# A gain vector brought to 128 partitions by two TensorE products instead of by a broadcasting load

## The chip, the cores and the metric

The kernel runs on one core of a Trainium2 chip. The metric is the device time of one execution in microseconds. The kernel before took 854.26 us, the median of three runs (853.2 to 855.99). One execution was also recorded by the hardware profiler; it took 853.36 us.

## The reference

One layer of an encoder trunk over 1536 tokens of 1024 features, in three groups of 512 tokens (a prompt of 1024 and a sample of 512):

```
h = rmsnorm(x, norm_g)            # x * rsqrt(mean(x*x) + 1e-6) * norm_g, per token over 1024 features
p = h @ w_in                      # 1024 x 4096, its columns split among three mixers
y = concat(conv branch, gated spatial branch, two-way recurrence)   # 256 + 256 + 512 wide
x = x + y @ w_out
out = rmsnorm(x, final_norm_g)
```

The change concerns norm_g alone, a vector of 1024 numbers that multiplies every token's features. Tokens lie on the 128 partitions while it is applied, so each partition needs the whole vector.

## The kernel before, in words

All products are made in float32 precision: a factor is split into a rounded part (hi, wh, hh) and a remainder (lo, wl, hl), and three products of such parts are summed (lines 204 to 206). ACT makes the rounded part, POOL or DVE the remainder.

At the start, `local_main` has SP issue the loads in this order: the first two chunks of 128 tokens (x00, x01), gb, two tiles of weights (wr), chunks 2 and 3, another weight tile, then the second group of tokens and the small parameter rows. The tile gb, 128 x 1024, is filled by one load that reads norm_g once for each partition, 512 KB (line 421).

The routine `prep` then turns token chunks into columns for the projection. For each chunk, ACT squares the tokens and sums them (`squares`, line 288), POOL makes the reciprocal root (lines 117 and 118), DVE multiplies the chunk by it and by gb (line 302), TensorE transposes it in eight blocks through two banks (tx, line 312), ACT evicts each bank rounded (hh, line 315) and DVE makes the remainder (hl, line 316). In between, `w_split` rounds the weights on ACT (wh, line 122) and makes their remainder on POOL (wl, line 123).

`prep` begins with `warm(18)`: 18 products of the identity with itself into a bank that nobody reads (line 216). Two more stand between the first two chunks. The first projection (pglu, lines 204 to 206) works on half a group, 256 tokens, at a time, so that it can start after two chunks; the transposes of chunks 2 and 3 stand in the middle of its products.

On ACT, DVE and POOL the instructions around the change run in the order in which the code is written. TensorE's stream is arranged by the framework's scheduler from the code and from what each instruction depends on. Each engine works through its own stream strictly in order and waits for the others by semaphores.

Of the kernel before, what the change touches and what calls it, by code (L numbers as in the profile page):

```python
# [11 lines left out]
F32 = mybir.dt.float32  # L12
# [3 lines left out]
AF = mybir.ActivationFunctionType  # L16
# [4 lines left out]
P = 128  # L21
DM = 1024
KT = DM // P
GRP = 512
# [9 lines left out]
WARM = (18, 2, 0)  # L34
# [21 lines left out]
def trunk_kernel(ctx, tc, x_prompt, x_sample, norm_g, w_in, conv_w, conv_b, conv_ln_g, conv_ln_b,  # L56
                 conv_pw, sgu_ln_g, sgu_ln_b, sgu_w, sgu_b, lb_fwd, lb_bwd, hgrn_norm_g, w_out,
                 final_norm_g, masks, y_prompt, y_sample):
    nc = tc.nc
    act = nc.scalar.activation  # L60
    dve = nc.vector
# [17 lines left out]
    def pj_t(name):  # L79
        return ps_pj.tile([P, GRP], F32, tag="pj", name=name)  # L80

    def tp_t(name):
        return ps_tp.tile([P, GRP], F32, tag="tp", name=name)

    def sc_t(name):
        return ps_sc.tile([P, NCH, P], F32, tag="sc", name=name)
# [4 lines left out]
    def uo_t(name):  # L91
        return ps_uo.tile([P, NCH, P], F32, tag="uo", name=name)
# [19 lines left out]
    def rstd(out, in_, n, mul=None):  # L112

        if mul is None:
            pool_e.tensor_scalar(out=out, in0=in_, scalar1=EPS, scalar2=None, op0=ALU.add)
        else:
            pool_e.tensor_scalar(out=out, in0=in_, scalar1=mul, scalar2=EPS, op0=ALU.mult, op1=ALU.add)
        pool_e.tensor_tensor(out=out, in0=out, in1=mexp[:, :n], op=ALU.pow)
# [93 lines left out]
    def warm(n):  # L212

        t = uo_t("warm").rearrange("p c n -> p (c n)")
        for _ in range(n):
            nc.tensor.matmul(t[:, :P], ident, ident, start=True, stop=True)
# [60 lines left out]
    def load_x(g, c, alloc):  # L277
        xt = alloc([P, DM], f"x{g}{c}")
        nc.sync.dma_start(xt, xsrc[g][c * P:(c + 1) * P, :])
        return xt  # L280

    def prep(xs, junk_t, gb):

        sts = {}

        def squares(g, c):
            st = sts[g, c] = const.tile([P, 1], F32, tag="st_x", name=f"st{g}{c}", bufs=4)
            act(junk_t(f"jx{g}{c}"), xs[g][c], AF.Square, accum_out=st)

        def by_pool(g, c):  # L290
            return g and c % 2 == 1

        def gained(g, c):
            pool_e.tensor_tensor(out=xs[g][c], in0=xs[g][c], in1=gb, op=ALU.mult)

        def scaled(g, c):
            xt, st = xs[g][c], sts[g, c]
            rstd(st, st, 1, 1.0 / DM)
            if by_pool(g, c):
                dve.tensor_scalar(out=xt, in0=xt, scalar1=st, scalar2=None, op0=ALU.mult)  # L300
            else:
                dve.scalar_tensor_tensor(out=xt, in0=xt, scalar=st, in1=gb, op0=ALU.mult, op1=ALU.mult)

        def turned(g, c):
            if c == 0:
                hts[g] = [[big.tile([P, 4, GRP], F32R, tag="H", name=f"h{e}{g}{a}") for a in range(2)] for e in "hl"]
            his, los = hts[g]
            xt = xs[g][c]
            for a in range(2):
                tp = tp_t(f"tx{g}{c}{a}") if a == 0 else sc_t(f"tx{g}{c}{a}").rearrange("p c n -> p (c n)")  # L310
                for k in range(4):
                    nc.tensor.transpose(tp[:, k * P:(k + 1) * P], xt[:, (4 * a + k) * P:(4 * a + k + 1) * P], ident)
                tp3 = tp.rearrange("p (k t) -> p k t", k=4)
                hi, lo = his[a][:, :, c * P:(c + 1) * P], los[a][:, :, c * P:(c + 1) * P]
                act(hi, tp3, AF.Copy)
                dve.tensor_tensor(out=lo, in0=tp3, in1=hi.bitcast(F32), op=ALU.subtract)
            ready[g] = c + 1

        warm(WARM[0])
        squares(0, 0)  # L320
        scaled(0, 0)
        squares(0, 1)
        scaled(0, 1)
        w_split()
        turned(0, 0)
        warm(WARM[1])
        turned(0, 1)
        warm(WARM[2])
        squares(0, 2)
        scaled(0, 2)  # L330
        squares(0, 3)
        scaled(0, 3)
        w_split()
        yield 4
        turned(0, 2)
        yield 2
        turned(0, 3)
        yield 1
        rest = [(g, c) for g in range(1, NG) for c in range(NCH)]
        for i in range(len(rest) + 2):  # L340
            if i < len(rest):
                squares(*rest[i])
            if 1 <= i <= len(rest):
                scaled(*rest[i - 1])
            if i < len(rest) and by_pool(*rest[i]):
                gained(*rest[i])
            if i >= 2:
                turned(*rest[i - 2])
            yield PACE
# [32 lines left out]
    def local_main(l1, accs):  # L382

        glus = [[l1.tile([P, len(gs) * GRP + 2 * PAD], F32, tag=f"glu{si}", name=f"glu{si}{i}", bufs=2)
                 for si, gs in enumerate(seqs)] for i in range(2)]
        gb = l1.tile([P, DM], F32, tag="gb", name="gb")

        def sg_t(name):
            return l1.tile([P, GRP], F32, tag="sg", name=name, bufs=3)

        def where(g):
            return (0, g) if g < 2 else (1, 0)

        def glu_pair(i, g, parts=(slice(0, GRP),)):
            sg = sg_t(f"sglu{i}{g}")

            def val_done(pj):
                si, j = where(g)
                dve.tensor_tensor(out=glus[i][si][:, PAD + j * GRP:PAD + (j + 1) * GRP], in0=pj, in1=sg, op=ALU.mult)

            pg, pv = pj_t(f"pglu{i}{g}"), pj_t(f"pval{i}{g}")
            for part in parts:
                last = g == NG - 1 and part.stop == GRP
                project(A_GLU + i, g, "", lambda pj: act(sg, pj, AF.Sigmoid), pg, part)
                if last:
                    w_split()
                project(A_VAL + i, g, "", val_done, pv, part)
                if last:
                    w_split()

        with tc.tile_pool(name="xp", bufs=1) as xp:
            def x_t(shape, name):
                return xp.tile(shape, F32, tag="x", name=name, bufs=9)

            def junk_t(name):
                return xp.tile([P, DM], BF16, tag="junk", name=name, bufs=2)

            xs = [[] for _ in range(NG)]
            xs[0].append(load_x(0, 0, x_t))
            xs[0].append(load_x(0, 1, x_t))  # L420
            nc.sync.dma_start(gb, norm_g.broadcast_to((P, DM)))
            w_load()
            w_load()
            for c in range(2, NCH):
                xs[0].append(load_x(0, c, x_t))
            w_load(x_t([P, KT, P], "wr2"))
            xs[1] = [load_x(1, c, x_t) for c in range(NCH)]
            rows = xp.tile([N_ROWS, P], F32, tag="rows", name="rows")
            for r0, src in ((R_NG, norm_g[0]), (R_CB, conv_b[0]), (R_CLG, conv_ln_g[0]), (R_CLB, conv_ln_b[0]),
                            (R_SLG, sgu_ln_g[0]), (R_LBF, lb_fwd[0]), (R_LBB, lb_bwd[0]), (R_HNG, hgrn_norm_g[0]),  # L430
                            (R_CW, conv_w[0].rearrange("a b -> (a b)"))):
                n = src.shape[0] // P
                nc.sync.dma_start(rows[r0:r0 + n, :], src.rearrange("(r j) -> r j", j=P))

            for i in range(2):
                for si, gs in enumerate(seqs):
                    pool_e.memset(glus[i][si][:, :PAD], 0.0)
                    pool_e.memset(glus[i][si][:, PAD + len(gs) * GRP:], 0.0)
            with tc.manual_schedule(engines={mybir.EngineType.Activation, mybir.EngineType.DVE,
                                             mybir.EngineType.Pool}):  # L440
                task = prep(xs, junk_t, gb)
                next(task)
                xs[2] = [load_x(2, c, x_t) for c in range(NCH)]
                spawn(task)
                for g in range(NG):
                    glu_pair(0, g, (slice(0, GRP // 2), slice(GRP // 2, GRP)))
            pp = tp_t("pp")
            nc.tensor.transpose(pp[:, :N_ROWS], rows, ident[:N_ROWS, :N_ROWS])
            dve.tensor_copy(par, pp[:, :N_ROWS])
        with tc.tile_pool(name="l2", bufs=1, reuse_waits="tile") as l2:  # L450
            with tc.manual_schedule(engines={mybir.EngineType.Activation, mybir.EngineType.DVE,
                                             mybir.EngineType.Pool}):
                local_rest(l2, accs, glus, glu_pair, where)
# [721 lines left out]
```

## Time and profile before

| | |
|---|---|
| time, median of three runs | 854.26 us (853.2 to 855.99) |
| the profiled execution | 853.36 us |
| its span, first to last instruction | 851.5 us |
| PE (TensorE products) busy | 824.1 us, 97% |
| DVE, ACT, POOL busy | 503.2, 348.6, 279.1 us (59%, 41%, 33%) |
| moved by DMA | 55.57 MB, mean 65 GB/s |
| mean granted TensorE clock | 0.993 |

A product of two float32 tiles shows as two records on PE, a transpose or a product of rounded parts as one. Records overlap, since products are pipelined; the spacing of their starts tells how fast they go, not the length of one. The time of a load is from its issue on SP's queue (SPq) to the moment at which a waiting engine goes on.

### The profile page before, as it was taken

The page shows a single profiled execution, that of the slowest core. Times are in us where ns is not written, and L with a number is a line of the kernel's source. Part 1 is how long each engine was busy: PE and PEld are TensorE (multiplying, and loading weights), DVE is VectorE, ACT ScalarE, POOL GpSimd, SP SyncE. Part 2 cuts the span into 40 slices and gives each one's busy share as a digit, 9 for nine tenths or more (in the row PEclk, how much of TensorE's full clock was granted, in tenths as well). Part 3 has the DMA queues.
Part 4 walks back from the last instruction along what each step waited for, and adds up shares of the span by engine and source line. Part 5 has one row for each costly group of instructions (what it writes and reads, how often), then busy time and mean ns, then how long its engine had stood idle before and what let it go on. Part 6 is the DMA issues. An engine that isn't in the chain of part 4 may idle for free.

```text
span 851.5 us, 17505 instructions
## 1 busy us (share of the span) xinstructions
PE 824.1 (97%) x7249; PEld 705.2 (83%) x7249; DVE 503.2 (59%) x1024; ACT 348.6 (41%) x707; POOL 279.1 (33%) x288
## 2 busy tenths in 40 slices
PE   7999999999999999999999999999999779999996
PEld 6998998787888889988878888998887667888886
DVE  4737789756323588631498748873227998443332
ACT  5724546541344354422345434442224555222221
POOL 5826766986142321220222032103113540101111
PEclk9999999999999999999999999999999899999999
DMA  7301201121020200101101011002212261334421
GB/s 273 138 16 42 75 2 49 50 64 62 25 62 13 75 27 3 49 28 38 50 27 39 2 38 48 19 2 63 75 36 87 79 210 51 126 130 144 146 99 50
DMA packets 56929, 55.57 MB, mean 65 GB/s; under 512 B 2875, under 2 KB 46226, under 8 KB 56850
## 3 DMA queue, kind: packets, MB, share of 16 engines
q1 hardware_dynamic: 56850, 54.45, 19.7%
q8 instruction: 57, 0.93, 0.5%
q14 instruction: 22, 0.18, 0.1%
HBM read 41.86 MB, written 12.58 MB: 64 GB/s over the span
## 4 chain that ended last, share of the span: by engine, by line
PE 83%; DVE 10%; ACT 2%; DMA 1%; POOL 1%; issue 1%; SPq 0%; POOLq 0%; ACTq 0%; DVEq 0%
PE pf L204 5%; PE po L1060 5%; PE po L1058 5%; PE pf L206 5%; PE pf L205 5%; PE po L1059 5%; DVE Q L765 4%; PE o L957 3%; PE pq L204 2%; DVE K L765 2%; PE sc L790 2%; PE pq L205 2%; PE pq L206 2%; PE U L890 2%; PE pg L204 2%; PE pg L205 2%
## 5 line engine op out<-in xcount | busy, mean ns | idle before, releaser
L123 POOL TENSOR_TENSOR wl<-wr,wh 128x512 fp32r<-128x512 f32 x64 | 85.5, 1349 | 162.4 <-ACT wh L122 162.4
L475 DVE SCALAR_TENSOR_TENSOR ca<-glu,par,ca 128x512 f32<-128x512 f32 x120 | 80.6, 748 | 0.0
L1058 PE MATMUL po<-woh,yh 128*128 128x512 f32 (+1 forms) x200 | 77.6, 388 | 0.8 <-ACT yh L1038 0.8
L1060 PE MATMUL po<-woh,yl 128*128 128x512 f32 (+1 forms) x200 | 76.5, 383 | 1.5 <-DVE yl L1039 1.5
L204 PE MATMUL pf<-hh,wh 128*128 128x512 f32 x192 | 76.8, 400 | 0.0
L1059 PE MATMUL po<-wol,yh 128*128 128x512 f32 (+1 forms) x200 | 76.2, 381 | 0.0
L206 PE MATMUL pf<-hh,wl 128*128 128x512 f32 x192 | 75.0, 391 | 0.0
L205 PE MATMUL pf<-hl,wh 128*128 128x512 f32 x192 | 74.8, 390 | 0.0
L771 ACT ACTIVATE kc<-K 128x512 f32<-128x512 f32 x84 | 56.4, 674 | 43.1 <-DVE K L765 40.4
L500 POOL TENSOR_TENSOR part<-part,pr 128x512 f32<-128x512 f32 x54 | 68.7, 1301 | 13.0 <-ACT pr L499 13.0
L765 DVE TENSOR_TENSOR Q<-Q,T 128x256 f32<-128x256 f32 x144 | 69.7, 525 | 2.0 <-ACT q L801 0.8
L765 DVE TENSOR_TENSOR K<-K,T 128x256 f32<-128x256 f32 x144 | 61.1, 465 | 5.8
L122 ACT ACTIVATE wh<-wr 128x512 fp32r<-128x512 f32 x64 | 39.0, 627 | 54.7 <-PE pf L205 20.6
L709 DVE TENSOR_SCALAR Q<-Q,oml,lbt 128x512 f32<-128x512 f32 x24 | 17.8, 742 | 64.8 <-ACT Q L706 64.8
L1064 DVE TENSOR_TENSOR yx<-po,yx 128x512 f32<-128x512 f32 (+1 forms) x25 | 16.7, 670 | 58.7 <-PE po L1060 58.7
L1060 PEld LDWEIGHTS po<-woh,yl 128*128 128x128 f32 x200 | 37.6, 188 | 9.2 <-DVE yl L1039 2.0
L1058 PEld LDWEIGHTS po<-woh,yh 128*128 128x128 f32 x200 | 37.6, 188 | 7.8 <-ACT yh L1038 0.9
L1059 PEld LDWEIGHTS po<-wol,yh 128*128 128x128 f32 x200 | 37.7, 188 | 6.8
L206 PEld LDWEIGHTS pf<-hh,wl 128*128 128x128 f32 x192 | 36.0, 188 | 7.8
L1076 POOL TENSOR_TENSOR stf<-stf 128x1 f32<-128x1 f32 x12 | 3.1, 261 | 119.0 <-ACT yx L1065 119.0
L204 PEld LDWEIGHTS pf<-hh,wh 128*128 128x128 f32 x192 | 36.1, 188 | 7.1
L205 PEld LDWEIGHTS pf<-hl,wh 128*128 128x128 f32 x192 | 36.1, 188 | 6.9
(366 smaller groups left out, 2265.1 us busy)
## 6 DMA issues: line engine op xcount, KB each, us to landing
wr<-in_w_in_dram SPq DMA_DIRECT2D x62, 256.0 KB
out_dram<-yx SPq DMA_DIRECT2D x24, 256.0 KB
yx<-yd SPq DMA_DIRECT2D x12, 448.0 KB
x<-in_x_prompt_dram SPq DMA_DIRECT2D x8, 512.0 KB
wor<-in_w_out_dram SPq DMA_DIRECT2D x8, 512.0 KB
yx<-in_x_prompt_dram SPq DMA_DIRECT2D x8, 512.0 KB
yd<-yc SPq DMA_DIRECT2D x12, 256.0 KB
x<-in_x_sample_dram SPq DMA_DIRECT2D x4, 512.0 KB
```

Of the source, the lines that this page charges most:

```text
L122: act(hi, src, AF.Copy)
L123: pool_e.tensor_tensor(out=lo, in0=src, in1=hi.bitcast(F32), op=ALU.subtract)
L204: nc.tensor.matmul(pj[:, part], hi[:, k, :], hh, start=k == 0, stop=False)
L205: nc.tensor.matmul(pj[:, part], hi[:, k, :], hl, start=False, stop=False)
L206: nc.tensor.matmul(pj[:, part], lo[:, k, :], hh, start=False, stop=k == KT - 1)
L475: dve.scalar_tensor_tensor(out=acc, in0=src, scalar=col(R_CW + 2 * t + i), in1=acc, op0=ALU.mult, op1=ALU.add)
L500: pool_e.tensor_tensor(out=parts[g], in0=parts[g], in1=pr, op=ALU.add)
L765: dve.tensor_tensor(out=x, in0=x, in1=y, op=ALU.mult)
L771: act(view(kc, 0, [[2 * m, n2], [m, 2], [1, m]]), view(K, 0, [[2 * m, n2], [GRP + m, 2], [1, m]]), AF.Copy)
L1058: nc.tensor.matmul(po, yh[:, k, :], hi[:, ns], start=k == 0, stop=False)
L1059: nc.tensor.matmul(po, yh[:, k, :], lo[:, ns], start=False, stop=False)
L1060: nc.tensor.matmul(po, yl[:, k, :], hi[:, ns], start=False, stop=k == KT - 1)
```

## The change

A row tile, grow, of one partition with 1024 numbers is loaded with norm_g (4 KB), as the second load instead of the third, between x00 and x01. A row of 128 ones is set by DVE. Two products of the ones, as the stationary factor, with a half of grow each, put 512 features of the vector on all 128 partitions of a bank (gp); they have one row of contraction each. ACT copies each bank into a half of gb. The 18 warm-up products are written as nine before and nine behind these products.

```diff
-    def prep(xs, junk_t, gb):
+    def prep(xs, junk_t, gb, ones, grow):
...
-        warm(WARM[0])
+        warm(WARM[0] // 2)
+
+        for a in range(2):
+            gp = tp_t(f"gp{a}")
+            nc.tensor.matmul(gp, ones, grow[:, a * GRP:(a + 1) * GRP], start=True, stop=True)
+            act(gb[:, a * GRP:(a + 1) * GRP], gp, AF.Copy)
+        warm(WARM[0] // 2)
         squares(0, 0)
         scaled(0, 0)
...
             xs[0].append(load_x(0, 0, x_t))
+            grow = xp.tile([1, DM], F32, tag="grow", name="grow")
+            nc.sync.dma_start(grow, norm_g[0:1, :])
             xs[0].append(load_x(0, 1, x_t))
-            nc.sync.dma_start(gb, norm_g.broadcast_to((P, DM)))
+            ones = xp.tile([1, P], F32, tag="ones", name="ones")
+            dve.memset(ones, 1.0)
             w_load()
             w_load()
```

The streams as the engines get them differ from the text of the code on TensorE. Its stream at the start of the program, before (warm is the warm-up product, tx a transpose, pglu the first projection):

```order
L1171 UNCONDITIONAL_BRANCH
L216 MATMUL warm<-ident 128x128 x18
L312 MATMUL tx_197<-ident,x_109 128x128 x4
L312 MATMUL tx_204<-ident,x_109 128x128 x4
L216 MATMUL warm<-ident 128x128 x2
L312 MATMUL tx_214<-ident,x_111 128x128 x4
L312 MATMUL tx_221<-ident,x_111 128x128 x4
L204 MATMUL pglu_260<-hh_193,wh_183 128x256
```

and now, where gp is a product of the ones with half the vector:

```order
L1180 UNCONDITIONAL_BRANCH
L323 MATMUL gp_165<-grow,ones 128x512
L323 MATMUL gp_168<-grow,ones 128x512
L216 MATMUL warm<-ident 128x128 x18
L312 MATMUL tx_207<-ident,x_109 128x128 x4
L312 MATMUL tx_214<-ident,x_109 128x128 x4
L216 MATMUL warm<-ident 128x128 x2
L312 MATMUL tx_224<-ident,x_113 128x128 x4
L312 MATMUL tx_231<-ident,x_113 128x128 x4
L204 MATMUL pglu_270<-hh_203,wh_193 128x256
```

Both gp products stand ahead of all 18 warm-up products, not between two halves of them; what follows is in the order of before.

ACT's stream at the start of the program, before:

```order
L288 ACT_TABLE_LOAD
L288 ACTIVATE jx_172,st_171<-x_109 128x1024
L288 ACTIVATE jx_178,st_177<-x_111 128x1024
L122 ACTIVATE wh_183<-wr_114 128x512
L122 ACTIVATE wh_183<-wr_116 128x512
L315 ACTIVATE hh_193<-tx_197 128x4x128
```

and now:

```order
L324 ACT_TABLE_LOAD
L324 ACTIVATE gb<-gp_165 128x512
L324 ACTIVATE gb<-gp_168 128x512
L288 ACTIVATE jx_182,st_181<-x_109 128x1024
L288 ACTIVATE jx_188,st_187<-x_113 128x1024
L122 ACTIVATE wh_193<-wr_117 128x512
L122 ACTIVATE wh_193<-wr_119 128x512
L315 ACTIVATE hh_203<-tx_207 128x4x128
```

The two copies of gp stand ahead of the squares of the first chunk.

## Rows read from the trace of the kernel before

**Rows 1.** The page: busy engines, and the chain that ended last by engine

```profile
PE 824.1 (97%) x7249; PEld 705.2 (83%) x7249; DVE 503.2 (59%) x1024; ACT 348.6 (41%) x707; POOL 279.1 (33%) x288
...
PE 83%; DVE 10%; ACT 2%; DMA 1%; POOL 1%; issue 1%; SPq 0%; POOLq 0%; ACTq 0%; DVEq 0%
```

**Rows 2.** The chain in order of time, 8 to 22 us: start, us, what

```profile
2.57 7.92 DMA wr<-in_w_in_dram
...
10.52 0.63 ACT wh L122
...
13.91 1.27 ACT jx L288 x3
...
17.08 2.30 DVE x L302
...
19.52 1.07 PE tx L312 x8
```

**Rows 3.** Timeline of ACT, first 30 us: start, us, instruction, [idle before, releaser]

```profile
4.45 1.06 ACT L288 ACTIVATE jx<-x 128x1024 bf16<-128x1024 f32 x1 [2.44 <-DMA x<-in_x_prompt_dram]
...
5.73 1.06 ACT L288 ACTIVATE jx<-x 128x1024 bf16<-128x1024 f32 x1
...
9.46 0.63 ACT L122 ACTIVATE wh<-wr 128x512 fp32r<-128x512 f32 x1 [2.58 <-DMA wr<-in_w_in_dram]
10.52 0.63 ACT L122 ACTIVATE wh<-wr 128x512 fp32r<-128x512 f32 x1 [0.43 <-DMA wr<-in_w_in_dram]
11.06 2.04 ACT L315 ACTIVATE hh<-tx 128x512 fp32r<-128x512 f32 x4
12.96 1.08 ACT L288 ACTIVATE jx<-x 128x1024 bf16<-128x1024 f32 x1
```

**Rows 4.** Timeline of POOL, first 30 us

```profile
5.68 0.19 POOL L117 TENSOR_SCALAR st<-st 128x1 f32<-128x1 f32 x1 [4.10 <-ACT jx L288]
5.95 0.56 POOL L118 TENSOR_TENSOR st<-st,mexp 128x1 f32<-128x1 f32 x1
```

**Rows 5.** Timeline of DVE, first 30 us

```profile
8.30 2.48 DVE L302 SCALAR_TENSOR_TENSOR x<-x,st,gb 128x1024 f32<-128x1024 f32 x2 [7.45 <-DMA gb<-in_norm_g_dram]
```

**Rows 6.** Timeline of PE, first 14 us

```profile
1.64 6.81 PE L216 MATMUL warm<-ident 128*128 128x128 f32 x36 [1.64 <-POOL ident masks.py:199]
9.64 1.09 PE L312 MATMUL tx<-ident,x 128*128 128x128 f32 x8 [1.19 <-DVE x L302]
10.57 0.61 PE L216 MATMUL warm<-ident 128*128 128x128 f32 x4
11.02 1.04 PE L312 MATMUL tx<-ident,x 128*128 128x128 f32 x8
```

**Rows 7.** Windows over the warm-up: stretch, length, PE busy (records), PEclk, DMA, GB/s

```profile
1.63:7.00 5.37, 5.37 (x25) 1.00 0.90 294
7.00:8.50 1.50, 1.45 (x13) 1.00 0.96 265
```

**Rows 8.** Timeline of SP's queue: issues of the first loads

```profile
0.72 0.86 SPq L279 DMA_DIRECT2D x<-in_x_prompt_dram  x2
1.63 0.42 SPq L421 DMA_DIRECT2D gb<-in_norm_g_dram  x1
2.10 1.08 SPq L178 DMA_DIRECT2D wr<-in_w_in_dram  x2
```

**Rows 9.** Windows of one us, columns as in rows 7

```profile
1.00:2.00 1.00, 0.36 (x1) 1.00 0.22 33
2.00:3.00 1.00, 1.00 (x6) 1.00 0.74 238
3.00:4.00 1.00, 1.00 (x7) 1.00 1.02 401
...
6.00:7.00 1.00, 1.00 (x7) 1.00 0.83 195
```

**Rows 10.** Waits over the whole span: us in total, times, longest

```profile
DVE ga L626 <- ACT ga L625: 9.1, 4, 4.3
```

More of the change, by code (lines that the diff above doesn't have):

```diff
@@ L440, in local_main @@
                                              mybir.EngineType.Pool}):
-                task = prep(xs, junk_t, gb)
+                task = prep(xs, junk_t, gb, ones, grow)
                 next(task)
```

## The prediction

> **What bounds the kernel now.** The page first: PE is busy for 97% of the span and the chain that ended last is 83% PE and 1% DMA [rows 1]. Then the chain in order of time over the first 22 us [rows 2], because the change sits there: it starts with the loads of the first projection weights, a wait of 7.92 us on wr until 10.52, and goes on over ACT's rounding of them (wh), ACT's evictions of the transposes (hh), the squares of the third token chunk (jx), and POOL and DVE's scaling, to the transposes at 19.52; from there PE works nearly without a gap. 7.92 of 851.5 us is 0.9%, so this one wait is nearly all the DMA in the whole chain. Behind it everything is written in program order on engines that wait for one another, and nothing waits for a clock on the wall. A shift of the opening therefore goes to the end one for one, in both directions.
>
> The opening itself is read engine by engine. ACT: x00 has landed at 4.45, squares of chunks 0 and 1 at 4.45 and 5.73, then idle until the weights land (9.46, 10.52), then four evictions and at 12.96 the squares of chunk 2 [rows 3]. POOL makes the first rstd by 6.51 [rows 4]. DVE could scale x00 then, but waits for the broadcast vector gb until 8.30 [rows 5]. PE runs 18 warm-up products (36 records) from 1.64 to 8.45 and the first transposes at 9.64 [rows 6]. The 12.96 is my mark: the third chunk's squares head the chain from there [rows 2], so its shift is the shift of the end.
>
> **What the change takes away.** The 512 KB of gb were third on SP's queue, ahead of both weight tiles [rows 8]. At 195 to 401 GB/s, the ends of the slices where it could run [rows 9], they are 1.3 to 2.7 us, by which the weights land sooner, and DVE loses its wait from 6.51 to 8.30. Alone that would be a gain of at most about 2 us. It counts only if what replaces gb is there in time.
>
> **What it puts in.** One 4 KB load, DVE's memset of 128 ones, four PE records and two ACT copies. The order of instructions decides: on PE both products stand ahead of all 18 warm-up products, and on ACT both copies stand ahead of the first squares. So PE no longer starts at 1.64 but when grow lands, and the 36 warm records, until now finished in an idle stretch, are queued behind the products and in front of the first transposes.
>
> Landing of grow: second on the queue, issued about 1.16, behind x00. Of x00's 524 KB, 33 + 238 KB had moved by 3.0 us and at 401 GB/s the rest by 3.63 [rows 9]; ACT saw it at 4.45 [rows 3], 0.8 us later. In line behind it I take 4.7. From the other side: x00's first bytes move about 1 us after its issue at 0.72 (33 GB/s in the second microsecond) [rows 8, 9]; a load that waited for nobody would be seen at 1.16 + 1.0 + 0.8 = 3.0. Later than 5.7 it can't be, since a 512 KB load in that place was seen by then [rows 3]. [...]
>
> Products: of the warm records 25 lie in 1.63 to 7.00, 215 ns each, and 13 in 7.00 to 8.50, 112 ns each [rows 7]. PEclk reads 1.00 in both, so the level has to be read from the spacing: it is half speed (1.2 GHz) first, then 2.4 GHz, and the engine had streamed without a gap since 1.64 when it rose. A product of 512 columns is also two records, of four times the columns: 0.86 us each at the lower level, 0.45 at the upper. PE now begins cold at 4.7: four records are 3.44 us, to 8.14. The first product is ready at 6.42 and the second at 8.14, each plus an estimated 0.2 to drain. The copies go by ACT's evictions of the same 128x512, four in 2.04 us, so 0.5 to 0.6 each [rows 3]: 6.6 to 7.2 and 8.35 to 8.95.
>
> ACT and DVE behind that: squares at 8.95 and 10.23 (pitch 1.28), the two wh from 11.5 to 12.75 (the weights have long landed). rstd of chunk 0: POOL begins 1.23 after the squares do and takes 0.83 [rows 4], 11.0; DVE's two scalings of 1.24 [rows 5], to 12.3 and 13.55. Chunk 1's transposes could start at 13.6, their first half is evicted from 14.2, and after two evictions the third squares start at 15.3: 2.35 us behind 12.96.
>
> PE behind that: I take the rise after the same stretch of streaming as before, 4.7 + 5.37 = 10.07. From 8.14 to there go 9 warm records at 215 ns, the other 27 at 112 ns take 3.02, to 13.1. The second nine products go to the same bank in a new tile and wait for the first nine to drain, 0.2 more: 13.3. Only then come the first transposes, against 9.64 before; x00 itself was scaled at 12.3. From the first transposes to the third squares it was 3.32 us, in which the weights held the first eviction back to 11.06 [rows 3, 6]. Without that hold: chunk 1's transposes 1.38 after chunk 0's, 0.6 until their first eviction, two evictions, 3.1 in all. 13.3 + 3.1 = 16.4, **3.4 us behind 12.96**. PE's side ends last, so this is the term; the gain of the removed transfer is swallowed, since both the weights and x00 wait for ACT and PE now.
>
> At nothing I count: the memset (DVE is idle until 8.30), the table load (one before, one after, still at the head of ACT while it waits), the SP issue (one for one), x01's issue 0.45 us later (its squares come at 10.23, not 5.73), and two waits on old transfers that move from an instruction of the gates to one two places earlier on DVE, since none of those waits was ever for a DMA [rows 10]. Not known is a matmul with one row of contraction; I take it at the speed of 128 rows.
>
> Sum: the profiled execution took 853.36, 853.36 + 3.4 = 856.8. The median of the runs shown, 854.26, is 0.9 higher and would give 857.7. I say 857.0.
>
> **Rivals.**
> 1. *The clock rises late* (0.17). If products with a single row do not bring the rise nearer, it comes 5.37 us after the first warm product, at 13.5: 25 records to there, 11 at 112 ns, transposes at 14.95, +5.1, **858.5**; if it stays low over the transposes too, about 860.5. For it: the only rise in the trace came under full products. Against: PE streams without a gap either way.
> 2. *Not slower: the vector is early* (0.22). Its place is the landing of grow, its price the 1.7 us between 4.7 and 3.0. With a landing at 3.0 the products end at 6.44, the rise comes at 8.37, the warm-ups end at 11.6, the third squares come at 14.7: +1.7, **855.1**. It turns into a gain only where PE also streams at the upper level from the start: products done at 4.8, copies at 5.6, third squares at 12.0 to 12.1, -0.9, **852.5**, the lowest that I can work out. For it: 4 KB is nothing beside 512. Against: x00's row, 3.7 us from issue to use, with one load in front of nothing. [...]
> 3. *The shift is given back later* (0.06): some stage behind 20 us has slack in absolute time. Then 853.4 to **854.5**. Against it stands the 1% DMA in the chain.
>
> **How the numbers follow.** The forecast's own case (0.55) runs from +2.35 (clock no limit, ACT and DVE end last) to +4.4 (landing at 5.7), so 855.7 to 857.8, a little more on the median. 0.3%, about what can be told from no change, is 2.6 us; some two thirds of this case lie beyond it. Slower: 0.55 x 0.65 + 0.16 = 0.52. Faster by over 2.6 us needs more than any case gives: 0.03. Same: 0.45. Range: from inside rival 2 to the first value of rival 1 and a little over, 854.0 to 859.2.
>
> **What would show it.** In the profile after: PE's first record waits for grow, near 4.7; four gp records near 0.86 us apart; 36 warm records from about 8.1 to 13.3 with the change of spacing inside; the first transposes near 13.3 and released by PE's own queue, not by DVE; ACT's squares at 8.95 and 15 to 16.4; no wait for wr. Wrong I would be if grow is seen by 3.5, if the spacing is 112 ns from the start, if DVE is what the first transposes wait for, or if PE's gaps behind 25 us shrink by the 3 us lost ahead of it.

## The result, and the profile after

The changed kernel takes 859.33 us (median of five runs, 858.37 to 859.59) against 854.26 us (853.04 to 855.99): the ratio is 1.0061 [1.0049, 1.0072], 5.1 us slower. The forecast was 857.0 with a range of 854.0 to 859.2. The direction was right, the size was short by 2.3 us, and the range missed the time by 0.13 us. The profiled execution took 859.42 us, its span is 857.6 us, and the mean granted TensorE clock is 0.992.

The page after, busy engines and the chain by engine, which answers to [rows 1]:

```profile
PE 828.0 (97%) x7253; PEld 706.3 (82%) x7253; DVE 504.4 (59%) x1025; ACT 349.7 (41%) x709; POOL 280.7 (33%) x288
...
PE 84%; DVE 10%; ACT 2%; POOL 1%; issue 1%; DMA 1%; POOLq 0%; ACTq 0%; SPq 0%; DVEq 0%
```

At this scale nothing is to be seen but 3.9 us more of PE, nearly all of it the four records of the two products (3.75 us below). The chain in order of time shows where it starts (start, us, what), beside [rows 2]:

```profile
1.16 3.45 DMA grow<-in_norm_g_dram
...
4.75 3.75 PE gp L323 x4
8.50 4.15 PE warm L216 x18
12.70 2.76 PE warm L216 x18
...
18.22 2.20 ACT jx L288 x4
```

The wait for the weights, 7.92 us of [rows 2], has left the chain. In its place stand the 4 KB load and 10.7 us of TensorE, the products and the warm-ups (4.75 to 15.45). TensorE's own timeline, for [rows 6]:

```profile
4.75 3.75 PE L323 MATMUL gp<-grow,ones 1*128 1x512 f32 x4 [4.75 <-DMA grow<-in_norm_g_dram]
8.43 7.03 PE L216 MATMUL warm<-ident 128*128 128x128 f32 x36
15.29 1.04 PE L312 MATMUL tx<-ident,x 128*128 128x128 f32 x8
...
16.61 1.04 PE L312 MATMUL tx<-ident,x 128*128 128x128 f32 x8
```

From 4.75 to the end of the second transposes the view shows no wait of PE for another engine; the first transposes are released by PE's own queue, at 15.29 where they stood at 9.64. How fast the warm-up went is read from the windows (stretch, length, busy and records, PEclk, DMA share, GB/s), as in [rows 7]:

```profile
8.43:12.25 3.82, 3.82 (x19) 1.00 1.05 356
...
13.80:15.30 1.50, 1.50 (x16) 1.00 1.04 415
```

3.82 / 19 is 0.20 us for a record, the lower level (1.2 GHz); 1.50 / 16 is 0.09, the upper (2.4 GHz). (The counts take in records that only reach into a window, so both come out a little short.) PEclk reads 1.00 in these rows, so it is again the spacing that tells them apart. The rise lies near 13.8, some 9 us after PE began to stream; before, it lay near 7.0, 5.4 us after [rows 6, 7].

ACT, for [rows 3]:

```profile
6.83 0.60 ACT L324 ACTIVATE gb<-gp 128x512 f32<-128x512 f32 x1 [4.83 <-PE gp L323]
8.53 0.60 ACT L324 ACTIVATE gb<-gp 128x512 f32<-128x512 f32 x1 [1.11 <-PE gp L323]
9.03 1.05 ACT L288 ACTIVATE jx<-x 128x1024 bf16<-128x1024 f32 x1
...
11.11 1.14 ACT L122 ACTIVATE wh<-wr 128x512 fp32r<-128x512 f32 x2
15.93 1.09 ACT L315 ACTIVATE hh<-tx 128x512 fp32r<-128x512 f32 x2 [3.68 <-PE tx L312]
...
18.22 1.06 ACT L288 ACTIVATE jx<-x 128x1024 bf16<-128x1024 f32 x1
```

The weights are rounded without a wait, and ACT then idles 3.68 us for the transposes. The mark, the third chunk's squares, is at 18.22 instead of 12.96: 5.26 us late.

DVE, and POOL, for [rows 5] and [rows 4]:

```profile
11.12 1.28 DVE L302 SCALAR_TENSOR_TENSOR x<-x,st,gb 128x1024 f32<-128x1024 f32 x1 [10.12 <-POOL st L118]
13.13 2.28 DVE L302 SCALAR_TENSOR_TENSOR x<-x,st,gb 128x1024 f32<-128x1024 f32 x1 [0.72 <-POOL st L118]
```

```profile
10.25 0.19 POOL L117 TENSOR_SCALAR st<-st 128x1 f32<-128x1 f32 x1 [8.67 <-ACT jx L288]
...
11.29 1.17 POOL L117 TENSOR_SCALAR st<-st 128x1 f32<-128x1 f32 x1 [0.20 <-ACT jx L288]
...
13.06 3.48 POOL L123 TENSOR_TENSOR wl<-wr,wh 128x512 fp32r<-128x512 f32 x2
```

The second chunk is scaled only by 15.41. The same 128x1 instruction on POOL takes 1.17 us while DVE scales and 0.19 alone, and DVE's scaling takes 2.28 us beside POOL's remainder of the weights and 1.28 without it. Here this hides behind PE (second transposes at 16.61); in an experiment below it doesn't.

Behind the mark the shift stays the same for a long while: the transposes that stood at 39.08 are at 44.34, again 5.26 late. Near 104 us a further 0.84 comes on top. ACT there waits longer for a weight tile, first before, then after (timelines of ACT):

```profile
97.55 0.63 ACT L122 ACTIVATE wh<-wr 128x512 fp32r<-128x512 f32 x1 [1.13 <-DMA wr<-in_w_in_dram]
```

```profile
103.89 0.63 ACT L122 ACTIVATE wh<-wr 128x512 fp32r<-128x512 f32 x1 [2.40 <-DMA wr<-in_w_in_dram]
```

and PE, which had no idle time there before, waits for that tile's remainder:

```profile
105.91 0.39 PE L230 MATMUL pbv0a<-wl,hh 128*128 128x256 f32 x1 [0.84 <-POOL wl L123]
```

5.26 + 0.84 = 6.10 is the whole difference of the two spans, 857.6 - 851.5. Between the medians it is 5.07, since the profiled execution of before was 0.9 below the median of its runs.

### The profile page after: what moved, and what is told of

It reads as the page before. It is cut to its first block, busy times and chain, and to the rows that moved or that the text cites. A ratio compares the mean times of both kernels' runs of the same rounds, so it can differ in the third digit from the quotient of the medians.

```text
span 857.6 us, 17515 instructions
## 1 busy us (share of the span) xinstructions
PE 828.0 (97%) x7253; PEld 706.3 (82%) x7253; DVE 504.4 (59%) x1025; ACT 349.7 (41%) x709; POOL 280.7 (33%) x288
## 4 chain that ended last, share of the span: by engine, by line
PE 84%; DVE 10%; ACT 2%; POOL 1%; issue 1%; DMA 1%; POOLq 0%; ACTq 0%; SPq 0%; DVEq 0%
PE pf L204 5%; PE po L1069 5%; PE po L1067 5%; PE pf L206 5%; PE pf L205 5%; PE po L1068 5%; DVE Q L774 4%; PE o L966 3%; DVE K L774 2%; PE pq L204 2%; PE sc L799 2%; PE U L899 2%; PE pq L205 2%; PE pq L206 2%; PE pg L204 2%; PE pg L205 2%
```

## The experiments

Two theories were set against each other. A: what sets the end is TensorE's queue, and in it the clock, whose rise products with one contraction row do not bring nearer. B: the clock is as forecast, and the loss sits elsewhere, on ACT, DVE and POOL or in the transfers. The mark is the third chunk's squares (12.96 before, 18.22 after). Where TensorE's order is given, the opening is written so that its instructions reach the engines as they stand in the code. Times are medians, against runs of the kernel before on the same chip (853.9 to 854.3); of each kernel one execution was profiled.

**One row or 128.** The same two products with the same number of columns, on the token tile that lands at the same moment, once with all 128 rows and once with one. TensorE's order is that of the change in both:

```diff
-            nc.tensor.matmul(gp, ones, grow[:, a * GRP:(a + 1) * GRP], ...)
+            nc.tensor.matmul(gp, ident, xs[0][0][:, a * GRP:(a + 1) * GRP], ...)       # full rows
+            nc.tensor.matmul(gp, ones, xs[0][0][0:1, a * GRP:(a + 1) * GRP], ...)      # one row
```

Full rows (the identity is the stationary factor here and x00 the moving one, where the expectation calls the identity moving):

> The two products ahead of the warm-ups get the same shape, place and copies, but full contraction: the identity as moving factor (512 columns of x00 against 128 rows) instead of one row of ones. gb then holds values of x00 instead of norm_g (that part of the computation is changed). Theory A, that a product with one row of contraction does not bring the rise of the TensorE clock nearer: the rise, 13.8 us in the changed kernel, comes about 5.4 us after the first product, near 10; the first transposes near 13.2 instead of 15.3, the third squares near 16.2 instead of 18.2, time 857.3 (2.0 under the changed kernel). Rival B, that the rise is late for another reason (the start at 4.75, the break between the two halves of the warm-up): the transposes stay at 15.3 and the time at 859.3.

One row:

> The twin of the full-row run: the moving factor is one row of x00 (512 columns) against the row of ones, so it differs from that run only in the rows, and from the changed kernel only in the numbers and in waiting for x00 instead of grow. gb holds values of x00 (that part of the computation is changed). Theory A: as the changed kernel, rise near 13.8, transposes at 15.0 to 15.3, 859.0 to 859.3. Rival B: the same as the full-row run, whatever that is.

Windows over the warm-up products with full rows, and then with one row:

```profile
8.10:9.30 1.20, 1.20 (x7) 1.00 1.06 411
9.30:13.00 3.70, 3.64 (x32) 1.00 1.09 359
```

```profile
8.25:9.30 1.05, 1.05 (x5) 1.00 1.04 417
9.30:13.20 3.90, 3.84 (x19) 1.00 1.08 360
13.20:14.80 1.60, 1.60 (x16) 1.00 1.02 407
```

With full rows the spacing falls to 0.116 us from about 9.3 on (3.70 / 32); with one row it stays at 0.205 to 13.2 and is 0.10 after. The products begin at 4.62 and 4.64 and take 3.75 us in both. This is the forecast's clock with full rows, and rival 1's with one. The twins differ in the rows and, bound up with them, in what the stationary factor holds, an identity or a row of ones; no run parts these two. The first transposes are at 13.11 and 14.91.

The time did not follow as expected: 859.2 (1.0063 [1.0048, 1.0078]) with full rows, 859.22 (1.0065 [1.0048, 1.0082]) with one. TensorE's timeline with full rows shows why the 1.8 us were not kept:

```profile
13.11 1.04 PE L312 MATMUL tx<-ident,x 128*128 128x128 f32 x8
...
15.34 1.09 PE L312 MATMUL tx<-ident,x 128*128 128x128 f32 x8 [0.75 <-DVE x L302]
...
23.54 1.94 PE L312 MATMUL tx<-ident,x 128*128 128x128 f32 x8 [1.71 <-DVE x L302]
```

The second chunk's scaling, slowed by POOL, ends last now (mark 17.00; with the 2.93 us that lie between first transposes and mark in the profile after, 13.11 would give 16.04), and after an idle stretch of 1.71 the clock has fallen: eight transposes take 1.94 instead of 1.06, the projection's products are 0.21 apart until 26.5, and the granted clock from 23.54 to 26.50 reads 0.50. At 44 us the two kernels are level, 4.87 and 4.88 behind before.

**The same with the other engines out of the way.** ACT's squares are put ahead of the copies, so that DVE needn't wait for POOL; TensorE's stream is that of the change, once with the one-row products and once with full rows:

```diff
+        squares(0, 0)
+        squares(0, 1)
         for a in range(2):
             gp = tp_t(f"gp{a}")
...
-        squares(0, 0)
         scaled(0, 0)
...
-        squares(0, 1)
```

One row:

> As the changed kernel on every engine but ACT, whose first two squares stand ahead of the two copies. Theory now: two limits lie over each other, (1) TensorE's queue, the warm-ups at half speed behind single-row products, and (2) ACT, whose squares wait behind the copies, so that POOL's second rstd and DVE's two scalings run into one another and into POOL's weight remainders (the second chunk scaled at 15.4, not 13.55 as forecast). This run takes away the second alone: chunks scaled by 10.5 and 12.7, but the first transposes stay at 15.3, the third squares at 18.2, time 859.3. Rival: ACT's order alone is the cause; third squares near 16, time 857.

Full rows:

> Both limits taken away: squares ahead of the copies, and the two products with full contraction (identity and x00), so that the clock rises near 9.3 as in the full-row run. gb holds values of x00 (that part of the computation is changed). Two limits: first transposes at 13.1 as there, but no wait for the second chunk's scaling (15.3 there), third squares near 16.2 instead of 17.0 (full rows alone) or 18.2 (squares first alone): 3.2 over the kernel before, 857.5 if the clock keeps its level over the transposes of chunk 3; if it falls there again as in the full-row run, about 0.9 more. Rival, that the end doesn't follow the opening one for one: 859 again.

With one row 859.36 (1.0058 [1.0043, 1.0073]): both chunks are scaled by 13.2, two microseconds sooner, the first transposes are still at 15.23, the mark at 18.15. So PE by itself is enough for the loss; theory B's engines were only hidden behind it. With full rows the rise is early again, near 10.2 against 13.7. In the same stretch of the warm-ups TensorE gets through 14 records with one row and 27 with full rows:

```profile
10.20:13.30 3.10, 3.04 (x14) 1.00 1.11 365
10.20:13.30 3.10, 3.04 (x27) 1.00 1.12 360
```

and the transposes with full rows are at:

```profile
13.38 1.04 PE L312 MATMUL tx<-ident,x 128*128 128x128 f32 x8
...
14.70 1.04 PE L312 MATMUL tx<-ident,x 128*128 128x128 f32 x8
```

Mark 16.30, 3.34 late: within 0.1 of the forecast's +3.4, though with another order on ACT, and the clock stays up over the fourth chunk's transposes. The time is 858.57 (1.0045 [1.0028, 1.0061]), 4.6 above before and not the 3.4 of the mark. The profiled execution (span 856.9, 5.4 above that of before) shows two places behind the mark. One is the later wait of after (0.85 on PE, at 103.99). The other, about 1.2, is a further fall of the clock near 679 (this run, then the same instructions in the profile after):

```profile
679.20:682.20 3.00, 3.00 (x12) 0.50 0.02 5
681.00:684.00 3.00, 3.00 (x17) 1.00 0.03 5
```

The profiles of two other kernels have it too, the one without warm-ups and the last one below, those of before and after do not; its cause is open. So the early rise is worth 1.85 at the mark (18.15 to 16.30), but its worth in time is not shown: the medians of the twins are 0.8 apart, and their intervals overlap.

**The products alone.** Before, with its broadcasting load, plus the 4 KB load and the two products at the head of TensorE's stream; nobody reads them and nothing is copied:

```diff
+            nc.sync.dma_start(grow, norm_g[0:1, :])
...
+        for a in range(2):
+            gp = tp_t(f"gp{a}")
+            nc.tensor.matmul(gp, ones, grow[:, a * GRP:(a + 1) * GRP], start=True, stop=True)
```

> One part of the change alone: the kernel before with its broadcasting load, plus the 4 KB load, the ones and the two products at the head of TensorE's stream, whose result nobody reads; no copies on ACT. If TensorE's queue is enough for the whole loss: first transposes at 15.2 as in the changed kernel, third squares at 18.2, 859.3. Rival, that the copies on ACT and the wait of DVE for them make the loss: DVE's scalings stay at 8.3, and the loss is smaller, 856 to 857.

859.05 (1.0061 [1.0048, 1.0074]). TensorE, and ACT:

```profile
4.64 3.75 PE L321 MATMUL gp<-grow,ones 1*128 1x512 f32 x4 [4.64 <-DMA grow<-in_norm_g_dram]
8.31 6.47 PE L216 MATMUL warm<-ident 128*128 128x128 f32 x36
14.63 1.04 PE L312 MATMUL tx<-ident,x 128*128 128x128 f32 x8
```

```profile
9.48 0.63 ACT L122 ACTIVATE wh<-wr 128x512 fp32r<-128x512 f32 x1 [2.54 <-DMA wr<-in_w_in_dram]
...
17.55 1.06 ACT L288 ACTIVATE jx<-x 128x1024 bf16<-128x1024 f32 x1
```

The weights come as late as before the change, ACT needs no copy, and by the median the loss is the whole of the change's all the same. The mark is 4.59 late instead of 5.26 (the rise comes near 12.6, so the transposes are at 14.63, not at the expected 15.2), and the later wait is there too (0.84). The loss is made in TensorE's queue.

**The load alone.** Before, without the broadcasting load; gb is set to ones by DVE:

```diff
-            nc.sync.dma_start(gb, norm_g.broadcast_to((P, DM)))
+            dve.memset(gb, 1.0)
```

> The other part alone: the kernel before without the 512 KB load and with nothing in its place but a memset of gb to 1.0 (the gain norm_g is left out). It gives the most that the removal can bring. By the sum of the prediction at most about 2 us: weights rounded from about 7.8 instead of 9.5, chunks scaled at 7.8 and 9.1, first transposes at 8.5, right behind the warm-ups, third squares at 11.6 instead of 13.0, 852.8. Rival, that the load was hidden anyway: no change, 854.2.

852.62 against 853.94 (12 runs; 0.9991 [0.9983, 1.0000]), mark 12.61, 0.35 early. The weights are rounded 2.6 and 2.75 us sooner (ACT's timeline), but then the transposes wait for DVE, whose second scaling takes 2.29 beside POOL again:

```profile
6.90 0.61 ACT L122 ACTIVATE wh<-wr 128x512 fp32r<-128x512 f32 x1
7.77 0.63 ACT L122 ACTIVATE wh<-wr 128x512 fp32r<-128x512 f32 x1 [0.26 <-DMA wr<-in_w_in_dram]
...
12.61 1.06 ACT L288 ACTIVATE jx<-x 128x1024 bf16<-128x1024 f32 x1
```

So what the change takes away was worth 1.3 us by the medians and 0.35 us by the mark; the interval runs from nothing to 1.5 us, so a gain is not clear of the noise.

**Order.** The change's code as it is written, nine warm-ups, the products, nine warm-ups:

```diff
-                next(task)
+                with tc.manual_schedule(engines={..., mybir.EngineType.PE}):
+                    next(task)
```

> TensorE's stream put into the order of the code's text: nine warm-ups, the two products, nine warm-ups. Nine warm-ups run from 1.64 to 5.5, the products from there at 0.9 per record to 9.1, copies to 9.8; ACT and DVE then end last (6.35 behind the copies), third squares near 16.1, time 857.2, if the single-row products only add nothing to the rise (rise near 10.6). Theory A in its stronger form, that they start it over: rise near 14.5, the nine late warm-ups and the first transposes at half speed, third squares 16.5 to 17, 857.6 to 858. Rival B, rise at 7.0 as in the kernel before: products done at 8.1, third squares 15.3, 856.4.

859.29 (1.0065 [1.0047, 1.0083]), mark 18.18. The windows over the first warm-ups, the products and the second warm-ups:

```profile
1.60:5.77 4.17, 4.14 (x18) 1.00 0.85 281
5.77:9.48 3.71, 3.71 (x6) 1.00 0.99 334
9.48:13.50 4.02, 4.02 (x19) 1.00 1.09 365
```

PE streams from 1.63 and is still at the lower level at 13.5 (4.02 / 19 = 0.21); the spacing changes near 14.2, within the first transposes (eight in 1.40 us from 13.51). So the 4.2 us of full products ahead of the one-row ones did nothing for the rise here, as theory A's stronger form had it (14.5). Its time, 857.6 to 858, was missed all the same: the second chunk's scaling ends last (second transposes at 16.52, after a wait of 1.17 for it), and the clock falls at the fourth chunk's transposes (1.94 us for eight at 24.71).

All 18 warm-ups ahead of the products, the squares ahead of the copies:

```diff
+        squares(0, 0)
+        squares(0, 1)
+        warm(18)
         for a in range(2):
```

> All 18 warm-ups ahead of the two products, as early as in the kernel before (1.64 to 8.45), squares ahead of the copies, nothing else between products and transposes. Rise at 7.0 as before; products at 8.3, 0.45 per record at the upper level, done at 10.1; copies to 10.9; chunks scaled at 12.2 and 13.5 to 14.5; transposes at 12.3 and 14; third squares near 16.0, +3.0, time 857.3. Rival, that single-row products let the clock fall: transposes at half speed, third squares near 17, 858.5.

858.74 (1.0052 [1.0037, 1.0067]). TensorE:

```profile
8.12 1.98 PE L324 MATMUL gp<-grow,ones 1*128 1x512 f32 x4
12.17 1.09 PE L312 MATMUL tx<-ident,x 128*128 128x128 f32 x8 [2.07 <-DVE x L302]
...
14.47 1.94 PE L312 MATMUL tx<-ident,x 128*128 128x128 f32 x8 [0.45 <-DVE x L302]
```

The products now run at the upper level, 1.98 us for the four records instead of 3.75. Behind them and an idle 2.07 us the first eight transposes still go at the upper level; it falls at about 13.3, and the projection runs at 0.21 us a product to 20.1. The mark is 16.94, 4.0 late. Whether the one-row products or the idle time let the level fall is not told apart by this run.

**No warm-up.**

```diff
-WARM = (18, 2, 0)
+WARM = (0, 2, 0)
```

> The 18 warm-up products are left out, all else as in the changed kernel. If the place of the warm-ups in front of the transposes is all that costs, the first transposes start when x00 is scaled, 12.4, the third squares come near 15.3, and the time is 856.5. By theory A the engine is then at half speed for the transposes and the first projection: chunk 1's second half is turned near 16.4, the third squares come near 17.0, and the projection's 23 products take about 4.9 us instead of 2.6, which brings the fourth chunk's transposes back to where they are in the changed kernel: 858.3 to 859.3.

858.7 (1.0062 [1.0045, 1.0079]). The transposes no longer queue behind warm-ups and start at 12.57, but both sets take 1.97 us, the projection is at the lower level until 21.0, and the mark is 18.07. The warm-up's queue and its absence cost about the same.

**Grow early.** A way out in the sense of rival 2, the vector early: the 4 KB are the first load, the products run before x00 is even there, six warm-ups follow, and ACT does squares, copy, squares, copy:

```diff
+            nc.sync.dma_start(grow, norm_g[0:1, :])
             xs[0].append(load_x(0, 0, x_t))
-            nc.sync.dma_start(grow, norm_g[0:1, :])
...
+        warm(6)
+        squares(0, 0)
+        act(gb[:, 0 * GRP:(0 + 1) * GRP], gps[0], AF.Copy)
+        squares(0, 1)
+        act(gb[:, 1 * GRP:(1 + 1) * GRP], gps[1], AF.Copy)
```

> The best guess from the two limits: grow is the first load (landing 2.5 to 3.0), the two products at once (to 6.5), six warm-ups behind them instead of 18, the first squares ahead of the first copy and the second squares ahead of the second copy. gb complete near 7.5, earlier than the broadcasting load brought it (8.30); chunks scaled at 8.8 and 10.1 to 11; transposes from 8.9 at half speed; third squares near 13.4, 0.4 over the kernel before. Time 854.5 if the clock rises before the projection, 855.5 to 857 if it stays low into it. Rival, that the warm-ups are needed whatever the order: 858 and more.

854.12 (ten runs; 1.0001 [0.9992, 1.0011]): the loss is gone, a gain isn't there. TensorE, and SP's queue:

```profile
2.43 3.75 PE L323 MATMUL gp<-grow,ones 1*128 1x512 f32 x4 [2.43 <-DMA grow<-in_norm_g_dram]
6.11 2.93 PE L216 MATMUL warm<-ident 128*128 128x128 f32 x12
9.38 1.97 PE L312 MATMUL tx<-ident,x 128*128 128x128 f32 x8 [0.34 <-DVE x L302]
```

```profile
0.72 0.36 SPq L427 DMA_DIRECT2D grow<-in_norm_g_dram  x1
```

With nothing ahead of it the load is seen 1.71 us after its issue; in the changed kernel, behind the 512 KB of x00, 3.59 us after. The DMA view of this run from 1.7 to 2.1 us holds two packets, one under 512 bytes and one of 2 to 8 KB: the 4 KB went as one piece, not spread over the 16 DMA engines. The transposes start at 9.38, before those of the kernel before, but at the lower level, and the mark is 13.70, 0.74 late. A last kernel had seven warm-ups there and none between the chunks:

```diff
-WARM = (18, 2, 0)
+WARM = (18, 0, 0)
...
-        warm(6)
+        warm(7)
```

> The early-grow version with seven warm-ups behind the products instead of six and without the two between the first two chunks, so that chunk 1's transposes no longer wait 0.9 us for these at half speed. Third squares near 13.2 (13.7 in the early-grow version, 12.96 in the kernel before), 853.8 if the clock rises near 11.3 as there. Rival, that the rise comes later without the two: projection at half speed, 855 to 856.

854.6 (1.0006 [0.9997, 1.0014]), no better: the mark is 13.25, but the clock falls at the transposes of the fourth chunk (1.78 us for eight at 19.78), and at 40 us it is 0.96 behind. No version that applies norm_g was faster than the kernel before.

## Why the prediction was right in direction and short in size

**What held.** Both products stand ahead of the warm-ups; grow was seen at 4.75 (4.7 forecast); the copies are at 6.83 and 8.53 (6.6 and 8.35), 1.70 apart for two product records, 0.85 each (0.86); the squares are at 9.03 and 10.07; no wait for the weights is left; the first transposes wait in PE's own queue. The load's removal alone is worth less than 2 us, and the TensorE queue swallows it. The landing was worked out from x00's rows and came out at 4.75; the early landing of rival 2 was not to be had behind x00, and with nothing ahead the load took 1.71 us, about the 1.8 that the rival reckons.

**The step that failed** is "I take the rise after the same stretch of streaming as before, 4.7 + 5.37 = 10.07". The runs show it near 13.8. The forecast had said that a product with one row was not known, and priced it at the speed of 128 rows: its duration came out (3.75 us with one row as with 128), its part in the clock did not. Two pairs of runs with one row and with 128 show it: the rise near 13.2 against 9.3, and near 13.7 against 10.2. Priced: the first transposes are at 15.29, not 13.3, which is 2.0 us; from there to the mark 2.93 were needed, not 3.1; so 18.22 stands where the forecast had 16.4. With full rows, and ACT's squares ahead of its copies, the mark is at 16.30. What the traces show is this shift of the mark; that the time of the kernel follows it is not shown, for neither pair of medians is apart beyond its intervals. Rival 1, "the clock rises late", had this as its mechanism, and nearly its numbers: transposes at 14.95, +5.1. I gave it 0.17 because PE streams without a gap either way; the pairs show that a busy record is no measure of what it does for the clock. "The only rise in the trace", said for that rival, was misread: the kernel before has another near 669 us (granted clock 0.50 from 666 to 669, 0.97 from 669 to 672), it too under products with all rows.

**A second term was mis-sized but hidden.** The second chunk's scaling was forecast to end at 13.55 and ended at 15.41, since POOL's and DVE's instructions, priced from rows where they ran alone [rows 4, 5], slow each other; the 2.30 of DVE's scaling in [rows 2] was at hand. It costs nothing in the changed kernel and 1.0 us at the mark (17.00 against 16.04) as soon as TensorE is quicker (the run with full rows and the change's ACT order). With it the forecast's ACT and DVE side would have ended near 17.0, behind PE's 16.4. That PE's side ends last, as forecast, was so only because the rise came late: in this the forecast was lucky. The rows read like one engine waiting for the other's instruction to end: POOL's began at 11.29 and ended at 12.46, right behind DVE's end at 12.40. The Trainium skill ("SBUF — State Buffer", SBUF: two separate sides) says that VectorE, in an operation with two SBUF inputs, and GpSimd, in one that reads SBUF, share a pair of ports that the first to start holds for its whole instruction. The trace agrees: of POOL's 1.17 us, 1.11 are what DVE's instruction had left. The forecast should have used it.

**"To the end one for one"** held for the first 100 us (5.26 at the mark, 5.26 at 44 us) and then a little was added, 0.84 us near 104: the second of two weight tiles was seen 5.80 us after their issue began, against 4.71 before. Of the nine kernels whose mark is over 3 us late, eight have it at 5.6 to 5.8; the ninth, without warm-ups and as late as the change itself, has it at 4.13, and the others have it at 4.1 to 4.7. So it does not follow from the delay alone, and its cause stays open. The forecast put everything behind the opening at nothing; without these 0.84 us the profiled execution would have come at 858.6, inside the range.

**The median.** 859.33 less 857.0 is 2.3 us: 1.8 of the mark and 0.84 of the later wait, less 0.3, since I had put 0.2 on the sum towards the median of before, and the profiled execution after is 0.1 above its own.

## What to carry to other kernels

What stands at the head of an engine's queue holds up all that stands behind it: ask what it waits for. Here TensorE stood until 4.75 for a 4 KB load. Moving the warm-ups ahead of the products (858.74) or leaving them out (858.7) gave nothing clear back; the kernel that loads the 4 KB first, with fewer warm-ups and with ACT's copies between its squares, gave the loss back (854.12), and no run parts these three. Products with one contraction row, as these runs show them, are to be priced as time in which the clock does not come nearer to its rise, even where PE is busy without a gap. A broadcast by TensorE is not free because it is small: here four records cost 3.75 us of the head of the queue, and a later rise, for a transfer whose removal was worth 1.5 us at most. Before pricing a removed transfer, run the kernel without it: that shows the most that its removal can bring.

## What the runs showed of the hardware that was not expected

- One-row products: PE is busy without a gap, yet the rise comes as late as if PE had begun only after them (13.2 against 9.3, and 13.7 against 10.2), and in the order of the code the 4.2 us of full products ahead of them brought it no nearer (14.2).
- The clock can fall again in an idle stretch of 1.7 us, but not always: in the kernel with full rows, in that with the code's order and in the last one the eight transposes behind such a stretch took 1.78 to 1.94 us, in nine others, behind the same 1.7, 1.06 or 1.07. What tells these cases apart was not found.
- The clock can also be low with PE busy throughout: 0.50 from 679.20 to 682.20 in the kernel with full rows and squares first, where the profile after has 1.00.
- The 4 KB load of one row went as one packet, and was seen 1.71 us after its issue with nothing ahead of it.
- An instruction of 128x1 on POOL is stretched sixfold by a scaling on DVE that began first (0.19 to 1.17 us), in the run without the load fourfold (0.84).
- With grow between the two token loads, the second chunk was seen at 7.44 to 7.52 in the three kernels with ACT's squares first and no broadcasting load, where ACT waited for it; before the change its squares ran at 5.73 [rows 3]. In the kernel with the products alone, with the same order of these loads, it was seen at 5.79. It is hidden in the changed kernel, whose second squares come at 10.07, and its cause is open.
